# RWKV-7 recurrence of a two-block network: chunk-local products ahead of the steps, outputs in two passes

## The chip, the cores and the metric

The kernel runs on one core of a Trainium2 chip. The metric is the device time of one execution in microseconds (us), the median of several runs.

## The reference, cut to what matters

The whole program is a network of two blocks with mixture-of-experts stages for 512 tokens of 1024 features. The change touches one part, the RWKV-7 recurrence in the first mixer. For each head (8 heads of size 64) and each of two directions it is:

```python
def step(s, inp):
    r_t, w_t, k_t, v_t, kk_t, b_t = inp
    sa = jnp.einsum('dbhvk,dbhk->dbhv', s, -kk_t)
    s = s * w_t[..., None, :] + sa[..., None] * b_t[..., None, :] + v_t[..., None] * k_t[..., None, :]
    return s, jnp.einsum('dbhvk,dbhk->dbhv', s, r_t)

_, ys = lax.scan(step, s0, xs)
```

The outputs of both directions are summed, normed by group, and gated. Gated linear attention, the out projection, the experts, and the second block follow or run beside it.

## The kernel before, in words

`phase1` builds the first mixer. It treats the heads in four pairs, `rwkv_pair(0)` to `rwkv_pair(3)`, and between them it emits pieces of gated linear attention (`gl(n)`, with L608, L663, L676 and others) and of an unrelated table of modulations (`fill(n)`, with L881, L891 and L897). The code is written with a framework that plans the order of every engine's queue ahead of time: among instructions that are ready by its own estimate it prefers those emitted first. On the chip each engine then works through its queue in that order, and waits on semaphores. So pieces of attention, fill and the next pair's projections (L307) stand in TensorE's queue between the parts of a pair.

A pair is computed in 8 chunks of 64 tokens. After projections, decays and scores, a triangular solve on VectorE (L483, L484) gives `UV` (with the state-free part of U) and `W`. Then come the sums `GQ` (L532 on TensorE, L535 and L536 on VectorE), the steps over the chunks, and the outputs.

Steps (L538 to L548): state `St[n + 1]` is decay times (G times state n, plus a product of the chunk alone). For each of 7 steps n, 2 directions d and 2 heads h, L545 multiplies `RN` and `UV` with all 128 rows (tiling 128x64: 128 rows of the array, 64 columns), and L547 adds G times `St[n]` to it in the same accumulator with 64 rows (tiling 64x64). L548 on VectorE then multiplies the whole 128x128 result by the decays into `St[n + 1]`. The accumulator `pc` has the tag "ch", of which there is one PSUM bank, taken anew every four steps.

Outputs (L549 to L560): for each chunk j and head h, up to four products are added up in one bank: two of `RN` and `UV` (one for each direction, 128x64), and one or two of `GQ` and `St` (64x64). A copy on ScalarE (L560) brings them to `Y`, and the group norm, gate and transposition follow (L564 to L589). L580, also 128x64, makes the gate's projection in another bank. The tag "sc" has three banks in rotation; the sums of L532, the outputs, L580 and L585 all take theirs from it.

Tiles of one tag are handed out in the order of the program. `t2` (6 tiles) is used by a pair's preparation (first by L357) and by its end (L567, L586).

A float32 product of TensorE is two matmul instructions in the profile.

Of the kernel before, what the change touches and what calls it, by code (L numbers as in the profile page):

```python
# [14 lines left out]
OP = mybir.AluOpType  # L15
# [3 lines left out]
T, D = 512, 1024  # L19
NT, KT = 4, 8  # L20
# [3 lines left out]
# ---------------------------------------------------------------- host layout  # L24
class Cols:
    """Vectors of 128*n features as columns [128, n] of one array."""
# [14 lines left out]
def lay_out(I):  # L41
    A = {}
# [7 lines left out]
    tiles = lambda v, n: v.reshape(KT, 128, -1, n).transpose(2, 1, 0, 3)    # [column tile, partition, k, n]  # L50
# [23 lines left out]
    # ---- second block  # L74
# [21 lines left out]
    # block-diagonal gate weights, two heads a tile: [direction, r or i, tile]  # L96
# [28 lines left out]
    # constants of the shapes alone: positions, window and the transforms at the frequencies pi (2 m + 1) / 1024  # L125
    # (even positions before odd ones, and each frequency's mirror image in the second half)
# [14 lines left out]
    # rows that lie along the free dimension: [2 heads of a pair, pairs * head size]  # L141
# [6 lines left out]
# ---------------------------------------------------------------- helpers  # L148
# [15 lines left out]
class Either:  # L164
    """tiles of some tags from a pool, all others from another"""
# [8 lines left out]
class Kern:  # L174
# [9 lines left out]
    # ------------------------------------------------------------ constants  # L184
    def consts(self):
# [6 lines left out]
        # 1 where partition == column  # L192
# [10 lines left out]
        self.beforeb = p([128, 128], "beforeb", mybir.dt.bfloat16)   # 1 where partition < column  # L203
# [5 lines left out]
        self.ident2 = p([128, 64], "ident2")                         # 1 where partition % 64 == column  # L209
# [4 lines left out]
    def rstd(self, x, out, width, junk):  # L214
        """out[128, NT] = rsqrt(mean(x^2) + eps) of x [128, NT, width]"""
        nc = self.nc
        ss = self.sp([128, NT], "ss")
        for t in range(NT):
            nc.scalar.activation(junk, x[:, t], AF.Square, accum_out=ss[:, t:t + 1])
        nc.scalar.activation(ss, ss, AF.Sqrt, scale=1.0 / width, bias=self.eps)  # L220
        nc.vector.reciprocal(out, ss)

    # ------------------------------------------------------------ phase 1
    def phase1(self, _):
        """first mixer: RWKV-7 in chunks of 64, pair of heads by pair, and gated linear attention"""
# [3 lines left out]
        with ExitStack() as es:  # L229
# [15 lines left out]
            # constants of this phase  # L245
            bones = X["bones"] = P([128, 128], "bones")         # 1 where both in the same head of a pair
# [3 lines left out]
            # masks over [s, (a t | r t)], per direction: what a token takes from another of its chunk  # L250
# [10 lines left out]
            keep = P([128, 8, 64], "keep")                      # 0 at the start of every chunk  # L261
# [3 lines left out]
            omm = P([128, 15], "omm")                           # 1 - mu, mu / 2  # L265
# [3 lines left out]
            hb = X["hb"] = P([128, 16], "hb")                   # halves of the gates' biases  # L269
            V.tensor_scalar(hb, c("rw_w0_f", 0, 16), 0.5, None, op0=OP.mult)  # L270
            ka = X["ka"] = P([128, 2, 4], "ka")                 # k_a / 2, 1 - k_a / 2
# [11 lines left out]
            # ---- x, its norm, and h = rmsnorm(x) with features on partitions  # L283
# [28 lines left out]
            def shifted(ft, out):  # L312
                """out = p + mu * (centred_shift(p) - p) of feature tile ft of the projections p"""
# [32 lines left out]
    def rwkv_pair(self, i, P, bank, S, t2, bones, mask, keep, hb, ka, rw_w2, rw_a2, rw_g2, lnr,  # L346
                  shifted, wl, al, gl, **_):
        """heads 2 i and 2 i + 1, on partitions (head, n) or (direction, token), in chunks j of 64 tokens.
        The state S obeys S' = decay (S + b U + k v), U = (I - L)^-1 (a S + ka v) in each chunk."""
# [18 lines left out]
        for d in range(2):  # L368
# [4 lines left out]
            sg = t2()                                   # 2 sigmoid  # L373
# [4 lines left out]
            a = t2()                                    # tanh, of which the gate is half of 1 +  # L378
            nc.scalar.activation(a, ps, AF.Tanh, scale=0.5, bias=hb[:, 8 + 4 * d + i:9 + 4 * d + i])
            # cumulative log decays inside chunks, in the direction's order  # L380
# [26 lines left out]
        # [U; v] of direction 0, [v; U] of direction 1: tokens on partitions, [head, chunk, v]  # L407
# [11 lines left out]
        # r . k of every token times its values  # L419
# [10 lines left out]
        # scores: of the tokens a, b (and k, on the other half) on partitions; and b, k themselves  # L430
        SA, RN = [], []
        for d in range(2):
            sa, rn = S("sa", 2, 8, 64), S("rn", 2, 8, 2, 64)
            for g in range(2):
                z = slice(4 * g, 4 * g + 4)
                # (rows of one head and of the other at once, so to different banks)
# [16 lines left out]
        # [ka v | a] with tokens on partitions  # L453
# [14 lines left out]
        # (I - L)^-1 of the two 32-blocks of every unit u = (head, chunk), by substitution with units on partitions,  # L468
        # where a unit's even and odd columns lie on two; direction 1 with rows and columns reversed
# [10 lines left out]
        nc.sync.dma_start(TT, A["c_eye"])             # the identity  # L480
# [12 lines left out]
        # the block between them, and the other, of zeros  # L493
# [19 lines left out]
        # U = U0 + W S  # L513
# [10 lines left out]
        # S' = decay (G S + [b; k] [U0; v]), outputs = [.; .] [U0; v] + Q S  # L524
        GQ = S("xa", 16, 2, 64).rearrange("p (d j) a n -> p d j a n", d=2)
        for d in range(2):
            gq = GQ[:, d]
            for g in range(2):
# [7 lines left out]
                V.tensor_add(gq[:, z, 1], ps[:, :, 1], self.ident2[:, None].to_broadcast([128, 4, 64]))  # L536
        St = S("TN", 8, 2, 64)
        for n in range(7):  # L538
            if n % 4 == 0:
                pc = bank("ch").rearrange("p (n d v) -> p n d v", n=4, d=2)  # L540
            for d in range(2):
                j = 7 - n if d else n
                for h in range(2):
                    o = pc[half[h], n % 4, d]
                    nc.tensor.matmul(o, RN[d][:, h, j, 1], UV[d][:, h, j], start=True, stop=n == 0)  # L545
                    if n:
                        nc.tensor.matmul(o, GQ[half[h], d, j, 1], St[half[h], n, d], start=False, stop=True)  # L547
            V.tensor_mul(St[:, n + 1], pc[:, n % 4], DC[:, :, n:n + 1].to_broadcast([128, 2, 64]))  # L548
        Y = S("tt", 8, 64)  # L549
        ps = bank("sc").rearrange("p (j v) -> p j v", j=8)  # L550
        for j in range(8):
            for h in range(2):
                mm = [(RN[d][:, h, j, 0], UV[d][:, h, j]) for d in range(2)]
                for d in range(2):
                    n = 7 - j if d else j
                    if n:
                        mm.append((GQ[half[h], d, j, 0], St[half[h], n, d]))
                for m, (l, rhs) in enumerate(mm):
                    nc.tensor.matmul(ps[half[h], j], l, rhs, start=m == 0, stop=m == len(mm) - 1)
        nc.scalar.copy(Y, ps)  # L560
        # group norm over each head, bonus, gate
# [30 lines left out]
    def gla(self, P, bank, S, load, project, hT, gla_gw2, mask, keep, **_):  # L592
# [6 lines left out]
        def token_major(out, src, act):  # L599
            """[(head, token), chunk, 128] of the 256 columns of a pair of heads"""  # L600
# [12 lines left out]
        for i in range(2):  # L613
# [12 lines left out]
            for d in range(2):  # L626
# [5 lines left out]
                # log sigmoid(z) = min(z, 0) - ln(1 + exp(-|z|))  # L632
# [47 lines left out]
            def silu(o, p):  # L680
                """2 silu"""
# [5 lines left out]
            # states that enter each chunk  # L687
            St = S("gs", 7, 2, 128)                       # (of direction 0 without the first, of 1 without the last)
# [36 lines left out]
            # half of 2 silu: 1 / (2 rms)  # L725
# [13 lines left out]
    def residual_open(self, es, w, nb, side="right"):  # L739
        """the pool of the residual's weights w, and the first of them as pairs of float32r parts"""  # L740
# [18 lines left out]
    def residual(self, M, bank, yT, q, brow, wr, ps_, mid=lambda: None):  # L759
        """xres += gate row q * (y @ w + brow); then, tile by tile of 128 tokens, x / rms(x) as two float32r parts that  # L760
# [1146 lines left out]
```

## Time and profile before

| | us |
|---|---|
| median of 3 runs | 3128.78 |
| lowest and highest run | 3128.35, 3137.92 |
| span of the profiled execution | 3136.6 |
| TensorE (PE) busy | 2830.5 |
| VectorE (DVE) busy | 1143.0 |
| ScalarE (ACT) busy | 719.4 |
| first mixer, to the last copy of pair 3 | 724.4 |

The span runs from the first to the last instruction of one profiled execution. Busy times are sums over all instructions of an engine. PE's matmuls overlap in its pipeline and their ends are modelled, so a run of them is best read by their starts. PEclk is the TensorE clock that was granted, as a share of 2.4 GHz; 0.50 is 1.2 GHz. A row in order of time that ends in "x4" merges four instructions of one line; a bracket holds the idle time of the engine before it and what ended it.

### The profile page before, as it was taken

What the parts mean: (1) busy time and instruction counts of PE and PEld (TensorE: products, weight loads), DVE (VectorE), ACT (ScalarE), POOL (GpSimd) and SP (SyncE); (2) the same over time, 40 slices, a digit from 0 to 9 for tenths busy, and PEclk for the clock granted to TensorE, in tenths of its full rate; (3) what the DMA queues carried; (4) which work ended last, traced back from release to release, by engine and by line L of the source; (5) the groups of instructions that cost most, each with busy time, mean ns of one, the idle gap of its engine ahead of it and who ended that gap; (6) DMA issues with size and microseconds to landing.
All of it is one profiled execution on the core that took longest, in us unless ns stands there. A gap on an engine that the chain in (4) does not pass through costs nothing. (4 is left out here: it accounts for less than half of the span.)

```text
span 3136.6 us, 39504 instructions
## 1 busy us (share of the span) xinstructions
PE 2830.5 (90%) x16658; PEld 1572.0 (50%) x16658; DVE 1143.0 (36%) x1998; ACT 719.4 (23%) x1192; POOL 291.4 (9%) x265
## 2 busy tenths in 40 slices
PE   7999999867889999999889969999998886999997
PEld 3565756655545444555556653333336663333333
DVE  4756272743312222233467541112115743121112
ACT  4223122412211111244355120110104331101001
POOL 1010010102000010000245200000003230000000
PEclk9999699957889999999889979999999887999999
DMA  4245254005669787987412339999992227999987
GB/s 139 88 129 169 69 168 135 16 8 193 235 236 336 269 309 291 321 292 279 157 62 97 131 142 405 400 409 380 381 381 81 81 88 301 409 401 381 409 337 301
DMA packets 270468, 738.25 MB, mean 235 GB/s; under 512 B 14860, under 2 KB 65292, under 8 KB 269393
## 3 DMA queue, kind: packets, MB, share of 16 engines
q1 hardware_dynamic: 260480, 711.77, 60.9%
q10 hardware_dynamic: 8176, 22.27, 2.0%
q8 instruction: 132, 2.16, 0.3%
q0 software_dynamic: 1632, 1.65, 0.2%
q14 instruction: 48, 0.39, 0.0%
HBM read 727.24 MB, written 8.40 MB: 235 GB/s over the span
## 5 line engine op out<-in xcount | busy, mean ns | idle before, releaser
L1475 PE MATMUL G<-w,xT 128*64 128x256 f32 (+1 forms) x4096 | 758.3, 494 | 0.0
L1475 PEld LDWEIGHTS G<-w,xT 128*64 128x64 f32 x4096 | 279.7, 137 | 370.6 <-issue 307.5
L1495 PE MATMUL Y<-w,hT 128*64 128x512 f32 x1472 | 440.4, 600 | 0.4 <-ACT hT L1486 0.4
L1495 PEld LDWEIGHTS Y<-w,hT 128*64 128x64 f32 x1472 | 141.3, 136 | 213.7 <-issue 200.7
L1646 DVE TENSOR_TENSOR xres<-xres,cb 128x512 f32<-128x512 f32 x238 | 163.3, 686 | 207.2 <-PE cb L1644 207.0
L1480 DVE TENSOR_TENSOR h<-h,G 128x256 f32<-128x256 f32 (+1 forms) x64 | 35.5, 555 | 519.4 <-PE G L1475 394.5
L1452 PE MATMUL gat<-oh,xhi 128*128 128x256 f32 x512 | 151.5, 322 | 15.7 <-DVE oh L1666 8.7
L827 POOL TENSOR_TENSOR wl<-ws,wh 128x1024 fp32r<-128x1024 f32 x36 | 88.8, 2471 | 666.5 <-ACT wh L826 646.6
L1452 PEld LDWEIGHTS gat<-oh,xhi 128*128 128x128 f32 x512 | 102.6, 200 | 87.0 <-issue 46.3
L1635 DVE SCALAR_TENSOR_TENSOR y<-Y,gate,g 128x512 f32<-128x512 f32 x32 | 24.0, 751 | 332.1 <-PE Y L1495 330.5
L1452 PE MATMUL gat<-oh,xlo 128*128 128x256 f32 x512 | 138.4, 297 | 0.0
L1644 PE MATMUL cb<-yhi,ohT 128*128 128x512 f32 x236 | 118.8, 503 | 15.6 <-ACT yhi L1636 9.7
L1644 PEld LDWEIGHTS cb<-yhi,ohT 128*128 128x128 f32 x236 | 44.4, 188 | 152.0 <-DVE xres L1646 85.1
L307 PE MATMUL mm<-hT,w 128*128 128x512 f32 x240 | 115.9, 612 | 0.0
L1452 PEld LDWEIGHTS gat<-oh,xlo 128*128 128x128 f32 x512 | 103.5, 202 | 15.9 <-issue 14.7
L1479 ACT ACTIVATE h<-G 128x256 f32<-128x256 f32 (+1 forms) x64 | 31.4, 491 | 317.4 <-PE G L1475 317.3
L1644 PE MATMUL cb<-ylo,ohT 128*128 128x512 f32 x236 | 99.9, 423 | 3.3 <-DVE ylo L1637 2.7
L916 ACT ACTIVATE xT<-gat,mods 128x256 f32<-128x256 f32 x64 | 36.1, 564 | 247.6 <-PE gat L1452 207.4
L1182 PE MATMUL b<-big,wh 128*128 128x512 f32 x320 | 86.8, 423 | 5.0 <-ACT wh L826 2.6
L1486 ACT COPY hT<-tr 128x256 f32<-128x256 f32 (+1 forms) x64 | 30.6, 479 | 243.3 <-PE tr L1485 243.3
L881 PE MATMUL ad<-wm,sc 128*32 128x256 f32 x768 | 68.8, 401 | 12.8 <-DVE rows L892 6.1
L1636 ACT CAST yhi<-y 128x512 fp32r<-128x512 f32 x30 | 18.5, 618 | 265.6 <-DVE y L1635 167.0
(631 smaller groups left out, 4113.7 us busy)
## 6 DMA issues: line engine op xcount, KB each, us to landing
w<-in_exp_w_dram SPq DMA_DIRECT2D x384, 1024.0 KB, 13.0
w<-in_moe_w_gate_dram SPq DMA_DIRECT2D x64, 1024.0 KB, 8.0
w<-in_moe_w_up_dram SPq DMA_DIRECT2D x64, 1024.0 KB, 7.3
w<-in_moe_w_down_dram SPq DMA_DIRECT2D x56, 1024.0 KB, 6.8
wm<-in_w_mod_dram SPq DMA_DIRECT2D x96, 512.0 KB, 4.3
ws<-in_w_in_dram SPq DMA_DIRECT2D x20, 512.0 KB, 3.2
ws<-in_cf_w_dram SPq DMA_DIRECT2D x20, 512.0 KB, 3.4
st<-in_w_out_dram SPq DMA_DIRECT2D x16, 512.0 KB, 4.8
```

The source lines that it names most:

```text
L307: nc.tensor.matmul(ps[:m], w[:, k, col0:col0 + m], hT[:, k], start=k == 0, stop=k == KT - 1)
L827: self.nc.gpsimd.tensor_sub(lo, x, hi.bitcast(F32))
L881: nc.tensor.matmul(ps[32 * k:32 * k + 32, 0:256], self.sc[:, 4 * g + k], ws[g][:, k], start=g == 0, stop=g == 1)
L916: self.nc.scalar.activation(out, ps, AF.Identity, scale=a, bias=b)
L1182: nc.tensor.matmul(ps, a[:, k], b[:, k], start=m == 0 and k == 0, stop=m == 2 and k == KT - 1)
L1452: nc.tensor.matmul(ps, part[:, t, 128 * k:128 * k + 128], oh[:, t], start=t == 0 and m == 0, stop=t == NT - 1 and m == 1)
L1475: nc.tensor.matmul(parts[m][64 * c:64 * c + 64], xT[:, k, 64 * e:64 * e + 64], w[:, kk, H * c:H * c + H], start=k == 0, stop=k == KT - 1)
L1479: nc.scalar.activation(h, parts[0], AF.Silu)
L1480: nc.vector.tensor_mul(h, h, parts[1])
L1495: nc.tensor.matmul(ys[n][64 * e:64 * e + 64], hTs[e][:, f], ws[e][:, ff_, 512 * n:512 * n + 512], start=f == 0, stop=f == nf - 1)
L1644: nc.tensor.matmul(ps, ohT[:m, 128 * t:128 * t + 128], p[k][:m], start=k == 0, stop=k == 1)
L1646: V.tensor_add(xr, xr, ps)
```

## The change

The products of `RN` and `UV` of all seven steps are made first, in two banks of tag "sc", and two multiplications on VectorE put them, times their decays, into `St`. Each of the steps 1 to 6 then holds four products of `GQ` and `St`, with no accumulation across tilings, and one multiply-add on VectorE for each direction adds decay times the result to what already lies in `St[n + 1]`. `pc` is taken anew every three steps. The outputs are made in two passes with a bank each: the products of `RN` and `UV` of all chunks, copied to `Y` by ScalarE, and then the products of `GQ` and `St`, added to `Y` by VectorE. No product is added or dropped. All other differences between the two files are comments.

```diff
         St = S("TN", 8, 2, 64)
-        for n in range(7):
-            if n % 4 == 0:
+        for g in range(2):
+            ps = bank("sc").rearrange("p (n d v) -> p n d v", n=4, d=2)
+            m = range(4 * g, min(7, 4 * g + 4))
+            for n in m:
+                for d in range(2):
+                    j = 7 - n if d else n
+                    for h in range(2):
+                        nc.tensor.matmul(ps[half[h], n % 4, d], RN[d][:, h, j, 1], UV[d][:, h, j], start=True, stop=True)
+            z = slice(m[0], m[-1] + 1)
+            V.tensor_mul(St[:, m[0] + 1:m[-1] + 2], ps[:, 0:len(m)], DC[:, :, z].rearrange("p d n -> p n d")[:, :, :, None]
+                         .to_broadcast([128, len(m), 2, 64]))
+        for n in range(1, 7):
+            if n % 3 == 1:
                 pc = bank("ch").rearrange("p (n d v) -> p n d v", n=4, d=2)
             for d in range(2):
-                j = 7 - n if d else n
                 for h in range(2):
-                    o = pc[half[h], n % 4, d]
-                    nc.tensor.matmul(o, RN[d][:, h, j, 1], UV[d][:, h, j], start=True, stop=n == 0)
-                    if n:
-                        nc.tensor.matmul(o, GQ[half[h], d, j, 1], St[half[h], n, d], start=False, stop=True)
-            V.tensor_mul(St[:, n + 1], pc[:, n % 4], DC[:, :, n:n + 1].to_broadcast([128, 2, 64]))
+                    nc.tensor.matmul(pc[half[h], n % 3, d], GQ[half[h], d, 7 - n if d else n, 1], St[half[h], n, d],
+                                     start=True, stop=True)
+            for d in range(2):
+                s = St[:, n + 1, d]
+                V.scalar_tensor_tensor(s, pc[:, n % 3, d], DC[:, d, n:n + 1], s, op0=OP.mult, op1=OP.add)
         Y = S("tt", 8, 64)
         ps = bank("sc").rearrange("p (j v) -> p j v", j=8)
         for j in range(8):
             for h in range(2):
-                mm = [(RN[d][:, h, j, 0], UV[d][:, h, j]) for d in range(2)]
                 for d in range(2):
-                    n = 7 - j if d else j
-                    if n:
-                        mm.append((GQ[half[h], d, j, 0], St[half[h], n, d]))
+                    nc.tensor.matmul(ps[half[h], j], RN[d][:, h, j, 0], UV[d][:, h, j], start=d == 0, stop=d == 1)
+        nc.scalar.copy(Y, ps)
+        ps = bank("sc").rearrange("p (j v) -> p j v", j=8)
+        for j in range(8):
+            for h in range(2):
+                mm = [(GQ[half[h], d, j, 0], St[half[h], n, d]) for d, n in ((0, j), (1, 7 - j)) if n]
                 for m, (l, rhs) in enumerate(mm):
                     nc.tensor.matmul(ps[half[h], j], l, rhs, start=m == 0, stop=m == len(mm) - 1)
-        nc.scalar.copy(Y, ps)
-        # group norm over each head, bonus, gate
+        V.tensor_add(Y, Y, ps)
```

## Rows read from the trace of the kernel before

**Rows 1.** The page: span and busy time of each engine.
```profile
span 3136.6 us, 39504 instructions
...
PE 2830.5 (90%) x16658; PEld 1572.0 (50%) x16658; DVE 1143.0 (36%) x1998; ACT 719.4 (23%) x1192; POOL 291.4 (9%) x265
```

**Rows 2.** Table of stretches: us; PE, PEld, DVE, ACT, POOL busy; clock, DMA.
```profile
153.90:183.00 29.10, 29.10 (x255) 20.13 (x253) 2.18 (x10) 0.37 (x1) 0.00 (x0) 1.00 0.20 65
307.80:352.90 45.10, 45.10 (x302) 33.62 (x301) 3.13 (x8) 0.59 (x1) 0.00 (x0) 0.50 0.05 18
490.10:519.00 28.90, 28.90 (x278) 21.10 (x275) 2.07 (x8) 0.37 (x1) 0.00 (x0) 1.00 0.21 65
674.50:712.60 38.10, 36.16 (x222) 27.08 (x219) 1.75 (x6) 0.00 (x0) 0.00 (x0) 0.56 0.00 1
```

**Rows 3.** ACT in order of time: start us, us, what, idle before.
```profile
195.81 0.59 ACT L589 COPY t<-sc 128x512 f32<-128x512 f32 x1 [5.31 <-PE sc L585]
196.29 0.64 ACT L357 ACTIVATE t<-kk 128x512 f32<-128x512 f32 x1
```

**Rows 4.** PE in order of time, a step of pair 0.
```profile
156.82 0.33 PE L545 MATMUL ch<-uv,rn 128*64 128x64 f32 x2
157.08 0.32 PE L547 MATMUL ch<-TN,xa 64*64 64x64 f32 x2
...
158.88 0.64 PE L881 MATMUL ad<-wm,sc 128*32 128x256 f32 x8
```

**Rows 5.** PE in order of time, outputs of pairs 0 and 1.
```profile
171.90 0.33 PE L559 MATMUL sc<-TN,xa 64*64 64x64 f32 x2
...
173.16 0.44 PE L559 MATMUL sc<-TN,xa 64*64 64x64 f32 x4
...
182.12 0.33 PE L559 MATMUL sc<-TN,xa 64*64 64x64 f32 x2
...
183.00 0.63 PE L881 MATMUL ad<-wm,sc 128*32 128x256 f32 x6
...
334.59 0.47 PE L559 MATMUL sc<-TN,xa 64*64 64x64 f32 x2
...
336.63 0.69 PE L559 MATMUL sc<-TN,xa 64*64 64x64 f32 x4
...
351.43 0.47 PE L559 MATMUL sc<-TN,xa 64*64 64x64 f32 x2
...
352.85 7.32 PE L608 MATMUL g<-wb,hT 128*64 128x128 f32 x84
```

**Rows 6.** L580: two runs in order of time; its duration (min/median/max).
```profile
153.07 0.98 PE L580 MATMUL sc<-rw_g,lora 128*64 128x64 f32 x25
...
306.25 1.75 PE L580 MATMUL sc<-rw_g,lora 128*64 128x64 f32 x25
...
L580 PE MATMUL sc<-rw_g,lora x128: 222/222/368, 153.0 to 676.7; 128*64 128x64 f32 x128
```

**Rows 7.** PE and DVE in order of time, a step of pair 3.
```profile
690.57 0.47 PE L545 MATMUL ch<-uv,rn 128*64 128x64 f32 x2 [0.38 <-DVE TN L548]
...
693.39 0.47 PE L547 MATMUL ch<-TN,xa 64*64 64x64 f32 x2
...
693.90 0.29 DVE L548 TENSOR_TENSOR TN<-ch,DC 128x128 f32<-128x128 f32 x1 [3.39 <-PE ch L547]
```

**Rows 8.** DVE groups by line: busy us, mean ns, idle before.
```profile
L210 DVE TENSOR_TENSOR ident<-ident 128x64 f32<-128x64 f32 x1 | 0.2, 219 | 0.0
...
L548 DVE TENSOR_TENSOR TN<-ch,DC 128x128 f32<-128x128 f32 x28 | 8.1, 290 | 72.5 <-PE ch L547 72.5
...
L581 DVE TENSOR_TENSOR tt<-tt,sc 128x512 f32<-128x512 f32 x3 | 2.1, 687 | 0.1
```

**Rows 9.** Table of stretches: pair 1's clock falls and rises.
```profile
300.00:305.00 5.00, 3.51 (x56) 3.27 (x53) 2.86 (x8) 0.00 (x0) 0.49 (x1) 0.84 0.03 7
355.00:360.00 5.00, 5.00 (x68) 5.00 (x66) 1.78 (x4) 3.50 (x4) 1.40 (x2) 0.70 0.00 0
```

## Prediction

> **What bounds the kernel now.** I read the page first: TensorE (PE) is busy for 2830 of 3136.6 us [rows 1], so the question is what a change takes from PE's queue, and whether anything else would then come last. The four stretches that the change touches, one for each pair of heads, are in the table of stretches [rows 2]: 29.1, 45.1, 28.9 and 38.1 us, 141.2 us in all. In each of them PE is busy from end to end, or nearly so in the last (36.2 of 38.1), while VectorE (DVE) works about 2 us and ScalarE (ACT) under 1. PE alone sets their length. Does a shorter stretch move what follows? The square that opens the next pair's preparation (L357) starts on ACT at 196.29, straight behind the last copy of the pair before (L589, 195.81) [rows 3]: pair follows pair. Both views agree for pairs 0 to 2: PE is full, and the pairs form a chain.
>
> **Why PE is full there is seen in its order of time.** A float32 product is two instructions. In the steps, groups of two on the 128x64 tiling (L545) alternate with groups of two on 64x64 (L547). A step goes from 156.82 to 158.88 in eight groups, 0.2575 us a group [rows 4]. In the outputs (L559) groups of four alternate: 24 groups from 173.16 to 182.12, 0.373 us each [rows 5]; so two more instructions on the same tile cost 0.116 us. Where one tiling stays and only the half changes, 25 instructions of L580 take 0.98 us, of which the last one's own 0.222 us is tail: 0.0316 us each, 0.063 for two [rows 6]. The rest of a group, 0.2575 - 0.063 = 0.194 us, I call the price of a switch of tiling. Some stretches run at a granted clock of 0.50 (the level of 1.2 GHz) [rows 2]. There the same sums give 0.403 us for two (seven groups from 690.57 to 693.39), 0.617 for four (24 from 336.63 to 351.43), 0.0576 for one in a run ((1.75 - 0.368) / 24) and so 0.288 for a switch [rows 5 to 7]. A group of four without a switch is 0.063 + 0.116 = 0.179 us, at the lower level 0.115 + 0.214 = 0.329.
>
> **The change part by part.** The 224 instructions of a pair's steps and outputs stay; their order changes. So I subtract, for each pair, PE's own time after from that before.
>
> Before, at full clock: six steps of 2.06 and outputs from 171.90 to 183.00 make 12.4 + 11.1 = 23.5 us; the other 5.6 us of the stretch is fill (L580, L881 and others between the steps). At the lower level: 6 x 3.23 + 18.3 (334.59 to 352.85) = 37.7 us, with 7.4 of fill in pair 1.
>
> After, at full clock: the 24 products of the six steps in one run, 24 x 0.063 = 1.5; six steps of four groups, each with a switch in and one out because fill stands between steps, 6 x (4 x 0.063 + 2 x 0.194) = 3.8; first output pass, 16 groups of four, 2.9; second pass, 12 of four and four of two, 2.4; two more switches 0.4. Sum 11.0 us, a gain of 12.5 for each of pairs 0 and 2. At the lower level the same line gives 2.8 + 6.2 + 5.3 + 4.4 + 0.6 = 19.2, a gain of 18.5 for pair 1, if its clock is again at 0.50.
>
> DVE work added per pair: twelve 128x64 multiply-adds out of PSUM for six 128x128 multiplies, two scalings of all states in place of the first multiply, and an addition of 128x512 where ACT had a copy. No row has the 128x64 form from PSUM. The bounds are 0.219 us (128x64 between SBUF tiles, L210) and 0.290 (twice as wide, from PSUM, L548) [rows 8]; I take 0.21 for each of the two, 0.42 a step, nearest to the narrow row, since following DVE instructions overlap a little (pairs of 0.29 would be 0.58). The scaling is like L581, 0.687 us for 128x512. The final addition is of the same size, for an ACT copy of 0.59 (like L589 [rows 3]): 0.1 us, left out. In pairs 0 to 2 all this is hidden by fill, as DVE is free for 27 of 29 us; without that cover a step would be the chain below, 0.95 instead of 0.64, and each pair would lose 1.9 us.
>
> The Trainium skill, "VectorE: DVE Perf Modes", section "Rules for kernel authors", speaks against this part: it asks for as few chained DVE instructions as can be, since each flushes the pipe. By it alone every one of the 24 steps would pay the extra 0.13 us, 3 us in all, and the sum below would be 64 instead of 66.
>
> Pair 3 has no fill left, so its steps are a chain. Before, L545 waits 0.38 us for the multiply of the step before although its own operands are ready [rows 7]: writes to the bank wait for its reader. After, PE's four groups at full clock last 7 x 0.0316 + 0.222 = 0.44 us, then 0.04 to DVE (693.86 to 693.90), 0.42 there, and 0.05 back (what 0.38 leaves beside 0.04 and the multiply's 0.29): 0.95 us; at the lower level 1.28. With 0.69 for the first scaling, six steps, what of the first pass and its two switches is not covered by that scaling, the second pass and a tail: 0.7 + 5.7 + 2.6 + 2.4 + 0.3 = 11.7 us at full clock, 0.7 + 7.7 + 5.2 + 4.4 + 0.7 = 18.6 at the lower. The clock of this stretch was 0.56 on the mean [rows 2], with full clock in its first microseconds; I take the middle, 15.2, a gain of 22.9. What is late next is the tail of norms, the same as before.
>
> What else moves: the run of products needs two more "sc" banks of three in rotation. They come free as DVE reads the sums of G and Q, so a bank is there before the 0.69 us scaling ends; I put this at nothing, at most one scaling (0.7 us) a pair. No DMA is added. The loads queued on SP and the small ones on POOL keep their places, as no instruction of those queues is in the edited lines; stages behind start earlier as a whole.
>
> Sum: 12.5 + 18.5 + 12.5 + 22.9 = 66.4 us. The profiled execution, 3136.6 us, becomes 3070.2. It is 7.8 us longer than the median of the runs shown, 3128.78; less the same 7.8, the prediction is 3062 us.
>
> **The rivals.**
> Pair 1 at full clock. Its clock fell in 300:305, where PE was busy for 3.51 of 5 us, and came back in 355:360, behind the run of L608 from 352.85 [rows 5, 9]. The new order puts long runs of one tiling right behind the fall. Then 45.1 us become 11.0 + 7.4 x 0.0316 / 0.0576 = 15.1, a gain of 30.0: 11.5 more, 3051 us.
> Pairs 0 and 2 at the lower clock. Their alternating groups held 1.00 [rows 2]; with more of PE's time in waits for DVE they may not. Each gains 23.5 - 19.2 = 4.3 instead of 12.5, 16.4 us less: 3079 us. [...]
> Only the last pair counts. If PE's time in pairs 0 to 2 is only traded for waits at the solves on DVE, 23 us are left: 3106 us. For it: PE has room in later parts of pair 3; against it: PE is full through the stretches and L357 follows L589.
> The order doesn't come about. The planner fills each queue by readiness, and could weave the first pass between the L547 groups; then the switches stay: within 0.3% of 3128. Against it: L580 runs 25 at a time already [rows 6].
> Slower: the lower clock spreads. If the thinner steps drop the clock and it stays down through the dense projections and fill behind, their time doubles. It decides once 66 us of dense full-clock work runs at half; with two stretches of 40 us between pairs the time is 3062 + 80 = 3142 us. Against it: in 355:360 the clock rose within a few microseconds of dense work [rows 9].
>
> **How the numbers follow.** Forecast 0.45 (3062), pair 1 at full clock 0.20 (3051), pairs 0 and 2 at the lower 0.15 (3079), only the last pair 0.10 (3106), order not there 0.05 (3128), slower 0.05 (3142). The first four are all faster by more than 0.3% (9.4 us, about what a measurement of this kernel can tell from no change): 0.90; same 0.05; slower 0.05. The range takes in the first three with their bounds. Low: 3051, less 3.5 (pair 3 all at full clock), less 7 (step switches absent in pairs 0 to 2, 18 x 0.39), less 6 for waits such as the 1.5 us one of 300:305, one a pair: 3034. High: 3079, plus 3.4 (pair 3 all at the lower level), plus 3.8 (24 steps with 0.58 on DVE), plus the same 6: 3092. It leaves out 0.20.
>
> **What would show it.** In the changed profile the two output passes should be blocks of about 3 and 2.5 us at full clock, the L547 groups of a step should start 0.06 us apart, the four stretches should last some 17, 27, 16 and 15 us, and the last copy of pair 3 (L589, which ends at 724.4 now) should end near 658. The prediction is wrong if groups of one tiling still cost 0.25 us (then the switch is not the price), if PE waits between pairs grow by what the stretches lose, or if the granted clock is at 0.50 in stretches where it was 1.00.

## The result, and the profile after

The kernel after takes 3042.21 us (median of four runs, 3040.67 to 3054.99); the kernel before, run beside it, 3128.57 (median of four, 3118.65 to 3137.92). The ratio is 0.9737 with a 95% interval of 0.9699 to 0.9775: 86.4 us less (70 to 94). The forecast was 3062 with a range of 3034 to 3092. The profiled executions, on which the sums of the prediction rest, stand further apart: 3136.6 against 3041.3 us of span, 95.3. Fifteen more runs of the kernel before lie between 3109 and 3144 us: the five with a mean granted clock of 0.940 or more took 3109 to 3121, the other ten (0.932 to 0.937) 3123 to 3144; the profiled one of before (0.933) is among the slower.

The page of the kernel after, span and busy times, which answers to [rows 1]:

```profile
span 3041.3 us, 39560 instructions
PE 2735.9 (90%) x16658; PEld 1507.6 (50%) x16658; DVE 1153.3 (38%) x2030; ACT 719.2 (24%) x1192; POOL 292.1 (10%) x265
```

PE has as many instructions as before, 16658, and is busy for 94.6 us less; the span is 95.3 us shorter. DVE works 10.3 us more. Lines are a little further down in this kernel: products ahead L548, their scaling L550, products of a step L557, multiply-add L561, first output pass L567, second L574, its addition L575, gate L595 (was L580), last copy of a pair L604 (was L589), fill L896 (was L881).

The table of the four stretches (us; PE, PEld, DVE, ACT, POOL busy; clock, DMA), which answers to [rows 2]:

```profile
153.90:165.90 12.00, 12.00 (x217) 8.10 (x214) 4.39 (x19) 0.98 (x3) 0.00 (x0) 1.00 0.26 89
288.60:302.40 13.80, 13.09 (x250) 9.28 (x246) 8.73 (x24) 3.42 (x6) 0.00 (x0) 1.00 0.26 79
432.60:444.50 11.90, 11.90 (x260) 9.56 (x256) 4.41 (x16) 0.96 (x2) 0.00 (x0) 1.00 0.27 90
604.00:615.10 11.10, 9.37 (x198) 8.23 (x194) 4.09 (x14) 0.58 (x1) 0.00 (x0) 0.80 0.01 3
```

They were 29.1, 45.1, 28.9 and 38.1 us and are 12.0, 13.8, 11.9 and 11.1: 17.1, 31.3, 17.0 and 27.0 less, 92.4 in all. The windows don't hold quite the same work: 0.9 to 1.3 us of the products ahead lie in front of each of these, and in front of those of before lie the first step's products and most of the gate (1.2 us in pair 0, from 152.67; 2.2 in pair 1, from 305.60), so each difference is good to about 1 us. Read the clock too: it is at 1.00 in pair 1 and at 0.80 in pair 3, where it was 0.50 and 0.56.

PE in order of time through pair 0, which answers to [rows 4] and [rows 5] (start us, us, what):

```profile
152.57 1.85 PE L548 MATMUL sc<-uv,rn 128*64 128x64 f32 x56
154.26 0.28 PE L567 MATMUL sc<-uv,rn 128*64 128x64 f32 x2
154.52 0.45 PE L557 MATMUL ch<-TN,xa 64*64 64x64 f32 x8
154.90 0.92 PE L567 MATMUL sc<-uv,rn 128*64 128x64 f32 x24
...
163.90 1.90 PE L574 MATMUL sc<-TN,xa 64*64 64x64 f32 x56
165.72 0.98 PE L595 MATMUL sc<-rw_g,lora 128*64 128x64 f32 x26
```

What were alternating groups of four, 0.373 us each, are now runs of one tiling. The 56 instructions of the second pass are one run, which starts 1.82 us before what follows it: 0.030 us each with a last one of 0.222. The 64 of the first pass are no single block: the planner put them between the first four steps, as runs of 2, 24, 22 and 16.

ACT around the end of pair 0, which answers to [rows 3]:

```profile
177.79 0.58 ACT L604 COPY t<-sc 128x512 f32<-128x512 f32 x1 [3.46 <-PE sc L600]
178.28 0.63 ACT L357 ACTIVATE t<-kk 128x512 f32<-128x512 f32 x1
```

Still pair follows pair: L357 stands straight behind the last copy, now 18 us earlier. The last copy of pair 3 ends at 627.2 instead of 724.4, 97.2 us earlier, and the end of the kernel gets 95.3 of them.

PE and DVE in pair 3, which answers to [rows 7]:

```profile
608.44 0.45 PE L557 MATMUL ch<-TN,xa 64*64 64x64 f32 x8
608.93 0.47 DVE L561 SCALAR_TENSOR_TENSOR TN<-ch,DC,TN 128x64 f32<-128x64 f32 x2 [0.63 <-PE ch L557]
609.46 0.45 PE L557 MATMUL ch<-TN,xa 64*64 64x64 f32 x8 [0.57 <-DVE TN L561]
...
610.49 0.66 PE L557 MATMUL ch<-TN,xa 64*64 64x64 f32 x8 [0.58 <-DVE TN L561]
...
611.71 3.31 PE L574 MATMUL sc<-TN,xa 64*64 64x64 f32 x56 [0.57 <-DVE TN L561]
```

This is the chain that was foreseen: eight instructions 0.45, 0.04 to DVE, two multiply-adds 0.47, 0.06 back: 1.02 us a step. The second pass, at the lower clock by then, takes 3.2 us.

### The profile page after: what moved, and what is told of

Same layout as the page of the kernel before. It is cut to its first block, busy times and chain, and to the rows that moved or that the text cites. A ratio compares the mean times of both kernels' runs of the same rounds, so it can differ in the third digit from the quotient of the medians.

```text
span 3041.3 us, 39560 instructions
## 1 busy us (share of the span) xinstructions
PE 2735.9 (90%) x16658; PEld 1507.6 (50%) x16658; DVE 1153.3 (38%) x2030; ACT 719.2 (24%) x1192; POOL 292.1 (10%) x265
## 5 line engine op out<-in xcount | busy, mean ns | idle before, releaser
L896 PE MATMUL ad<-wm,sc 128*32 128x256 f32 x768 | 66.2, 402 | 12.6 <-DVE rows L907 6.3
```

Of the source, the lines that this page charges most:

```text
L896: nc.tensor.matmul(ps[32 * k:32 * k + 32, 0:256], self.sc[:, 4 * g + k], ws[g][:, k], start=g == 0, stop=g == 1)
```

## Experiments

Theory: what the change takes away is switches of tiling in PE's queue, and the clock of pair 1 and of pair 3 with them. Rivals: half of the change does all of it; it is the accumulation of both kinds of products in one bank that costs, not the switch; the clock of pair 1 is an accident of one execution; another order of the fill does as much.

### One half at a time

The steps of the kernel after with the outputs of the kernel before:

```diff
-        for j in range(8):
-            for h in range(2):
-                for d in range(2):
-                    nc.tensor.matmul(ps[half[h], j], RN[d][:, h, j, 0], UV[d][:, h, j], start=d == 0, stop=d == 1)
-        nc.scalar.copy(Y, ps)
...
+                mm = [(RN[d][:, h, j, 0], UV[d][:, h, j]) for d in range(2)]
+                for d in range(2):
+                    n = 7 - j if d else j
+                    if n:
+                        mm.append((GQ[half[h], d, j, 0], St[half[h], n, d]))
```

> Edit: the changed kernel with the outputs of the kernel before (one bank, groups of four that alternate between 128x64 and 64x64); products ahead and steps as in the changed kernel. Theory (the price lies in alternating tilings, wherever they alternate): each pair's outputs take 11.1 us at full clock again instead of 3.9, so some 7 us a pair more than the changed kernel, and about 12 where the clock is at 0.50: 3070 to 3085 us. Rival (the gain comes from the steps alone, because products no longer queue behind the reader of their bank): within 5 us of the changed kernel, 3042 us.

3077.65 us (3077.03 to 3078.32), ratio 0.985 (0.9811 to 0.9888). Its table of stretches:

```profile
154.00:175.60 21.60, 21.60 (x248) 14.57 (x246) 4.14 (x18) 0.37 (x1) 0.00 (x0) 1.00 0.26 86
298.00:317.70 19.70, 19.70 (x284) 14.99 (x280) 4.84 (x16) 0.96 (x2) 0.00 (x0) 1.00 0.22 68
443.20:463.50 20.30, 20.30 (x268) 15.43 (x266) 3.89 (x16) 0.37 (x1) 0.00 (x0) 1.00 0.20 66
624.80:650.00 25.20, 22.67 (x206) 17.98 (x202) 3.61 (x14) 0.01 (x1) 0.00 (x0) 0.63 0.00 1
```

The other way round, the steps of the kernel before with the outputs of the kernel after (the reverse diff, for the steps):

> Edit: the kernel before with the outputs of the changed kernel (two passes of one tiling each); steps with accumulation across tilings as before. Theory (alternating tilings): outputs of 11.1 us become 3.9 in pairs 0 and 2, of 18.3 become 6 to 7 in pairs 1 and 3: 3128 - 14 - 24 = 3090 us, and some 15 us less if pair 1 runs at full clock. Rival (the steps alone): within 5 us of 3128.

3071.23 us (3068.25 to 3083.13), ratio 0.984 (0.9795 to 0.9884). Its table of stretches:

```profile
156.50:176.00 19.50, 19.50 (x211) 13.45 (x210) 2.18 (x10) 0.96 (x2) 0.00 (x0) 1.00 0.17 55
296.00:314.90 18.90, 18.90 (x223) 14.31 (x224) 2.50 (x7) 3.73 (x5) 0.00 (x0) 0.95 0.00 1
450.20:468.80 18.60, 18.60 (x224) 13.88 (x224) 2.08 (x8) 0.96 (x2) 0.00 (x0) 1.00 0.19 58
624.20:644.80 20.60, 19.45 (x188) 14.99 (x188) 1.75 (x6) 0.59 (x1) 0.00 (x0) 0.73 0.01 2
```

Set against [rows 2], the steps bring 7.5 and the outputs 9.6 in pair 0; together that is the 17.1 of the whole change (each to about 1 us, as above). In pair 2 it is 8.6 and 10.3 (17.0 by the whole), in pair 3 12.9 and 17.5 (27.0). In pair 1 they bring 25.4 and 26.2, but the whole only 31.3: some 20 us stand in both. That is the clock. Either half alone had pair 1 at full clock, or nearly (0.95), and it can be gained only once. So both halves count, and a part of pair 1's gain doesn't hang on which switches went: with the old outputs, too, its clock was not down.

### Switch or accumulation

The kernel after with both passes in their own banks and with their own copy and addition, but their groups in turn, as the outputs of the kernel before had them:

```diff
+        p1, p2 = (bank("sc").rearrange("p (j v) -> p j v", j=8) for _ in range(2))
...
         for j in range(8):
             for h in range(2):
+                with (self.tc.issue_after(last) if last is not None else ExitStack()):
+                    for d in range(2):
+                        x = nc.tensor.matmul(p1[half[h], j], RN[d][:, h, j, 0], UV[d][:, h, j], start=d == 0, stop=d == 1)
...
+                with self.tc.issue_after(x.ins):
+                    for m, (l, rhs) in enumerate(mm):
+                        last = nc.tensor.matmul(p2[half[h], j], l, rhs, start=m == 0, stop=m == len(mm) - 1).ins
```

> Edit: the changed kernel with both output passes kept in their own banks, with the same copy and addition behind them, but queued so that a group of the first pass and a group of the second alternate. Nothing but the order on TensorE is undone. Theory (alternating tilings): groups of four take 0.37 us at full clock, the outputs 11 us instead of 1.95 + 1.90; 7 us a pair more than the changed kernel at full clock, about 14 for a pair at 0.50: 3070 to 3085 us. Rival (accumulating both kinds of product in one bank was what cost time): groups take 0.12 to 0.18 us and the time is within 8 us of 3042.

3080.09 us (3073.43 to 3085.24), ratio 0.9859 (0.9816 to 0.9901): with the steps alone changed it was 3077.65, so the two passes brought nothing that shows in this order. PE in order of time in pair 0:

```profile
168.24 0.45 PE L569 MATMUL sc<-uv,rn 128*64 128x64 f32 x4
168.62 0.44 PE L573 MATMUL sc<-TN,xa 64*64 64x64 f32 x4
168.99 0.45 PE L569 MATMUL sc<-uv,rn 128*64 128x64 f32 x4
```

Its table of stretches, the groups of pairs 0 and 3:

```profile
166.60:177.80 11.20, 11.20 (x119) 9.10 (x120) 1.50 (x2) 0.92 (x2) 0.00 (x0) 1.00 0.24 78
634.50:652.90 18.40, 18.35 (x118) 14.71 (x120) 0.00 (x0) 0.39 (x1) 0.00 (x0) 0.50 0.00 1
```

The groups start 0.373 us apart, as in [rows 5], and the outputs take 11.2 and 18.4 us as they did, though no product is added to one of another tiling any more. In the outputs the price is the alternation of tilings; for the steps the next run shows the same. The Trainium skill, "TensorEngine Tiling (Array Packing)", section "Key Properties", says that a change of tiling mode drains the TensorE; these rows agree in that each change costs time, and put a size to it.

### What a group costs, by its length

The kernel after with products of constants ahead of the first mixer, results unused: alternating groups of two, a straight run of one tiling, groups of two again, a run, groups of four on one half, a run, groups of eight with the halves in turn, a run.

```diff
+            wide = lambda h: nc.tensor.matmul(scratch[z[h], 0:64], bones[:, z[h]], bones[:, 0:64], start=True, stop=True)
+            square = lambda h: nc.tensor.matmul(scratch[z[h], 64:128], bones[z[h], z[h]], bones[z[h], 0:64], start=True, stop=True)
...
+            alternate(80, lambda g: [g % 2])
+            for g in range(160):
+                nc.tensor.matmul(scratch[z[g % 2], 128:192], bones[:, z[g % 2]], bones[:, 0:64], start=True, stop=True)
+            alternate(120, lambda g: [g % 2])
...
+            alternate(80, lambda g: [g % 2, g % 2])
...
+            alternate(40, lambda g: [0, 1, 0, 1])
```

> Edit: the changed kernel with products of constants at the start of the first mixer, into a bank that nobody reads; the rest is unchanged, and the time longer by the added run (some 100 us). In order: 80 groups of two instructions that alternate between 128x64 and 64x64; 320 instructions on 128x64 alone, changing the half at every product; 120 alternating groups of two; 240 on 128x64; 80 alternating groups of four; 240 on 128x64 with four on the same half in a row; 40 alternating groups of eight with four changes of half; 240 on 64x64. Theory (a price for each switch): at full clock 0.26 us for a group of two, 0.37 for four, 0.38 for eight; the runs 0.03 us an instruction. My prediction's price list says that four in a row on the same half cost 0.179 us; the changed kernel's first pass (24 in 0.85 us) says 0.12. Clock: if alternating groups by themselves neither raise nor lower the clock, the first 20 us stay at 0.50, and the later alternating stretches at 1.00; if they let it fall, the second alternating stretch (31 us) ends at 0.50; if they raise it like any product, the first stretch is at 1.00 after some microseconds.

PE in order of time (wide L252, square L253, straight runs L262 and L268), cut out of the middle of each part:

```profile
39.80 1.39 PE L262 MATMUL sc<-bones 128*64 128x64 f32 x42
...
46.83 0.33 PE L252 MATMUL sc<-bones 128*64 128x64 f32 x2
47.08 0.33 PE L253 MATMUL sc<-bones 64*64 64x64 f32 x2
...
109.97 0.44 PE L253 MATMUL sc<-bones 64*64 64x64 f32 x4
110.34 0.45 PE L252 MATMUL sc<-bones 128*64 128x64 f32 x4
...
132.79 1.39 PE L268 MATMUL sc<-bones 128*64 128x64 f32 x42
...
144.80 0.45 PE L253 MATMUL sc<-bones 64*64 64x64 f32 x8
145.18 0.45 PE L252 MATMUL sc<-bones 128*64 128x64 f32 x8
```

And the table of stretches of the same kernel: the second part with groups of two, from its start and later, and the groups of four:

```profile
45.00:50.00 5.00, 5.00 (x41) 3.69 (x40) 0.00 (x0) 0.00 (x0) 0.00 (x0) 1.00 0.01 3
55.00:90.00 35.00, 35.00 (x176) 24.79 (x178) 0.00 (x0) 0.00 (x0) 0.00 (x0) 0.50 0.00 1
100.00:128.00 28.00, 28.00 (x301) 22.91 (x302) 0.00 (x0) 0.00 (x0) 0.00 (x0) 1.00 0.01 2
```

At full clock an alternating group of two starts 0.257 us before the next (twenty of them from 45.03 to 50.16), one of four (on one half) 0.373, one of eight (halves in turn) 0.38. Nothing is accumulated here, and the groups of two take what they took in the steps before (0.2575): there, too, it was the alternation that cost. In a run an instruction takes (1.39 - 0.222) / 41 = 0.0285 us, and it is the same when four in a row lie on one half (L268). So the 0.116 us for two more on the same tile, which the prediction read from [rows 4, 5], is no property of the tile: it shows only between switches. Second, the clock. Steady groups of two, with PE busy for 35.00 of 35.00 us, went from 1.00 to 0.50 within some microseconds and stayed there; groups of four held 1.00 for 28 us. At the start of this execution the clock column can't be used: it reads 1.00 there, while the first eighty groups of two start 0.403 us apart (from 19.80 to 21.01 in three), the pace that goes with 0.50 later. By its starts the straight run of L262 behind them began at 0.055 us an instruction (34.32) and went at 0.0285 from about 37 us on. The products of constants make the total, 3178.81 us, no comparison.

### Why pair 1 stood at the lower clock

The kernel before with twelve dense products, results unused, ahead of pair 1's steps (`last` is the last product of L532):

```diff
+        if i == 1:
+            dummy = bank("ch")
+            with self.tc.issue_after(last.ins):
+                for _ in range(12):
+                    nc.tensor.matmul(dummy, ident, v, start=True, stop=True)
```

> The kernel before, and in pair 1 alone twelve dense products more (identity times v, 128x128 by 128x512, 24 instructions, results unused) in TensorE's queue behind the last sum of L532 and ahead of the steps. Such an instruction takes about 0.434 us at full clock, so they add 10.4 us at full clock and 20.8 at the lower one. The question is why the steps and outputs of pair 1 ran at a granted clock of 0.50 for 45 us before. Theory: the clock had fallen in the waits ahead of them, and groups of two that alternate with another tiling do not raise it again; a dense run ahead raises it, and then, as in pairs 0 and 2, the same instructions hold 1.00. It expects the granted clock at 1.00 in pair 1's steps and outputs, some 28 us for them instead of 45.1, the dense run itself 11 to 14 us, and a total 3 to 6 us below the kernel before. Rival: the alternating groups of two pull the clock down again within a few microseconds, as in the run of constants where they fell back to 0.403 us a group; then the stretch keeps some 40 to 45 us at 0.50 and the total is 8 to 13 us above the kernel before.

A single execution, 3123.86 us, beside runs of before from 3109 to 3144, so the total says little. Its steps and outputs in the table of stretches:

```profile
315.90:344.00 28.10, 28.07 (x324) 21.71 (x325) 3.24 (x9) 0.12 (x1) 0.00 (x0) 1.00 0.09 29
```

45.1 became 28.1 us with not one switch fewer: the clock alone was worth 17 us. But the dense products didn't have to raise it. PE's wait ahead of them was shorter this time and the clock was never down, so what is shown is that the old order holds full clock if it enters with it. What it does once the clock is down, and what the new order does, the next two ask: the same 80 groups of two, of constants, ahead of pair 1 in the kernel after and in the kernel before.

```diff
+        if i == 1:
+            dummy = bank("ch")
+            with self.tc.issue_after(last.ins):
+                for g in range(80):
+                    h = half[g // 2 % 2]
+                    w = ident[h] if g % 2 else ident
+                    nc.tensor.matmul(dummy[h, 64 * (g % 2):64 * (g % 2) + 64], w[:, h], bones[h, 0:64] if g % 2 else bones[:, 0:64], start=True, stop=True)
```

> The kernel after, and in pair 1 alone 80 groups of constants (results unused) behind the last sum of L532 and ahead of the products of the steps: groups of two 128x64 instructions that alternate with groups of two 64x64, as in the kernel before. They cost 80 x 0.2575 = 20.6 us at full clock and 80 x 0.403 = 32 at the lower one, and, by the run of constants, leave the granted clock at 0.50. The question is what the new order does when its stretch begins at the lower clock, which in the kernel after it never did. Theory: its runs of one tiling raise the clock as the straight runs of constants did, so that the 56 products of the steps still go at about 0.058 us each, and the rest of the stretch, or nearly all of it, at 1.00: 14 to 18 us for a stretch that took 13.8 at full clock. Rival: the steps between the runs hold it at the lower level, as the old order did for 45 us; then the stretch takes 24 to 28 us. The total is no evidence, some 20 to 30 us above 3042.

> The counterpart: the same 80 groups of constants at the same place of pair 1 in the kernel before. Theory: the steps and outputs that follow, with their alternating groups, stay at the lower clock from the first group to the last, some 45 us; the stretch of the kernel before was no accident of one execution, but what its order does once the clock is down. Rival: the fill between the steps raises the clock within the stretch, which then takes some 30 to 38 us.

The kernel after with them, PE in order of time (constants L547, products ahead L555, first pass L574), and then two rows of its table of stretches, of which the second goes from the first product to the last of the second pass:

```profile
282.39 30.79 PE L547 MATMUL ch<-bones,ident 128*64 128x64 f32 x160
313.11 3.06 PE L555 MATMUL sc<-uv,rn 128*64 128x64 f32 x56
316.00 0.28 PE L574 MATMUL sc<-uv,rn 128*64 128x64 f32 x2
```

```profile
315.00:320.00 5.00, 5.00 (x123) 4.53 (x121) 2.61 (x8) 0.19 (x1) 0.00 (x0) 0.92 0.02 3
...
313.10:327.90 14.80, 14.80 (x309) 11.78 (x308) 5.24 (x16) 1.52 (x3) 0.00 (x0) 0.91 0.23 71
```

The kernel before with them, the table of stretches from the first step to the last output:

```profile
332.30:377.10 44.80, 44.80 (x314) 33.86 (x313) 3.25 (x9) 0.00 (x0) 0.00 (x0) 0.50 0.06 18
```

This settles what either order does with a clock that is down. From the same lower clock the old order stays at 0.50 for 44.8 us, to its last group, and the new one is out of it within its 56 straight instructions (0.50 to 315.5, 1.00 from 316.0) and needs 14.8 us.

It doesn't settle why the clock was down in one kernel and not in the other. In the kernel before it fell at 303.5, within the last run of L532, which had begun behind a wait of 1.49 us; neither the rest of that run nor the 25 straight instructions of L580 [rows 6] raised it again:

```profile
302.18 3.49 PE L532 MATMUL sc<-rn,Lu 64*64 64x128 f32 x46 [1.49 <-DVE Lu L523]
```

In the kernel after the clock fell ahead of pair 1 too, as its table of stretches has it:

```profile
275.00:280.00 5.00, 2.94 (x48) 2.12 (x46) 2.24 (x6) 1.52 (x5) 0.87 (x1) 0.95 0.40 141
280.00:285.00 5.00, 5.00 (x40) 2.93 (x40) 1.51 (x4) 1.53 (x5) 0.48 (x1) 0.71 0.78 264
285.00:290.00 5.00, 4.83 (x122) 4.48 (x124) 4.49 (x11) 3.23 (x4) 0.48 (x1) 1.00 0.02 3
```

It answers to [rows 9]: the fall came earlier, and the clock was back at 1.00 by 283, some 4 us ahead of the first product ahead (287.39), while PE was at work on instructions that the order before has too. So in this execution it wasn't the new order that brought it back, and whether and when it falls there is not shown to depend on the order; what the new order changes is that a fall no longer costs the whole stretch. Only one execution of the kernel before was profiled. An estimate from [rows 2]: 45.1 us at 0.50 take 45.1 x 0.5 / 3136.6 = 0.007 off an execution's mean clock, which is about what parts 0.933 from 0.940 among the runs listed with the result. Beside an execution whose pair 1 holds full clock, as in the run with dense products, some 17 us of the gain would be missing. The Trainium skill, "TensorE: Matmul & The Clock Gate", section "Why this matters for your kernels", warns of idle gaps between bursts. Here PE was busy for 44.80 of 44.80 us at 0.50: without a gap in the profile, too, the clock can be down, where short groups of two tilings alternate.

### One bank or two in pair 3

```diff
-                pc = bank("ch").rearrange("p (n d v) -> p n d v", n=4, d=2)
+                pc = [bank(t).rearrange("p (n d v) -> p n d v", n=4, d=2) for t in ("ch", "ad" if i == 3 else "ch")[:1 + (i == 3)]]
...
```

> The kernel after, with the step accumulators of direction 1 in a bank of their own in pair 3 alone. A step of pair 3 took 1.02 us (starts 608.44, 609.46, 610.49), with TensorE idle for 0.57 until the second of the two multiply-adds ended. Theory: the next step's first product writes into the bank that the multiply-add of direction 1 still reads, so it waits for both; with two banks the products of direction 0 start when the first multiply-add has ended, and a step lasts about 0.75 us, pair 3's six steps 1.5 us less. Rival: it is the state that each direction needs and the turn-round between the engines, not the bank, and a step stays at 1.0 us. The total can show neither, 1.5 of 3042 us; the starts of the steps can.

PE in pair 3 in order of time:

```profile
609.63 0.33 PE L557 MATMUL ch<-TN,xa 64*64 64x64 f32 x4
609.89 0.33 PE L567 MATMUL sc<-uv,rn 128*64 128x64 f32 x2
610.15 0.33 PE L557 MATMUL ad<-TN,xa 64*64 64x64 f32 x4
...
610.79 0.33 PE L557 MATMUL ch<-TN,xa 64*64 64x64 f32 x4
```

A step takes 1.16 us here (from the first group in "ch" at 609.63 to the next at 610.79; the others 1.10 to 1.29), not 0.75 and not 1.0. With the directions apart the planner puts products of the first pass between them, so that a step has four switches instead of two, and no step is left that shows the bank alone. What the bank costs stays open; the attempt only shows how easily the switches come back. The time was 3042.37 us.

### Another order of the fill

In the kernel after TensorE is busy for 17.7 of the 40 us around pair 3's solve (560 to 600). Two kernels move the twelve pieces of fill ahead of pair 3, all or six of them, to the end of the phase, where the planner may draw them forward (shown is the one with six; the other leaves the line out):

```diff
-            fill(12)
+            fill(6)
```

> The kernel after, with the twelve pieces of the modulation table that are emitted ahead of pair 3 left to the end of the phase, so that they can lie beside pair 3's solve, steps and norms. In the kernel after TensorE has nothing for about 40 us around pair 3's solve (busy 0 of 5 us in 575:580 and 580:585, the clock at 0.50 from 560 on) and for its tail. Theory: the pieces (12 x 16 wide products of 128x256 and their sums, near 25 us of TensorE) fill these gaps, pair 3's whole chain starts earlier, and the total falls by 10 to 20 us, to 3022 to 3032. Rival: the DVE, ACT and DMA work of the pieces gets in between pair 3's chain, or the pieces run behind pair 3 anyway, and the total stays within 5 us of 3042 or rises.

> As the run with twelve pieces late, but six of the twelve stay ahead of pair 3. Theory: half of the gain, 5 to 10 us, unless what counts is only that the gap around the solve is filled, for which six pieces (some 12 us of TensorE) are enough; then it gains as much as twelve. Rival: no gain, 3042 within 5 us.

All twelve late: 3061.01 us (3058.59 to 3064.58), ratio 0.9794 (0.9736 to 0.9852), some 19 us slower than the kernel after. PE in order of time (fill L895, first product of the out projection L788):

```profile
613.75 1.08 PE L895 MATMUL ad<-wm,sc 128*32 128x256 f32 x8 [2.21 <-DMA wm<-in_w_mod_dram]
...
655.44 0.77 PE L788 MATMUL G<-wh,yh 128*128 128x512 f32 x1 [12.08 <-ACT yh L840]
```

Pair 3 does end sooner, but the fill runs on until 643.4, waiting for its loads and for ACT and DVE, and the out projection begins at 655.44 instead of 636.58. Six late: 3035.98 us (3035.07 to 3044.35), ratio 0.9719 (0.9661 to 0.9778). There the fill is through at 590.7, inside the solve, and the out projection begins at 630.7, 5.9 us earlier. That is the size of the difference to the kernel after (6.2 us), but the two intervals overlap, so that it isn't shown to be faster.

## Why the prediction was right, and where it was off

**The bound.** Right. PE's busy time and the span fell by the same (94.6 and 95.3 us), L357 still starts behind the last copy, and of the 97.2 us at the last copy of pair 3 95.3 reached the end. Behind the outputs of pair 3 stands the tail of norms as before: from 615.1 to the last copy's end at 627.2 it is 12.1 us, and was 11.8.

**The switch as the price.** Right as the cause, shown by the woven passes and by the groups of constants; its size was off, in two terms. Pair 0's own PE time was to be 11.0 us and is 8.4:

| us in pair 0 | prediction | starts in the trace after |
|---|---|---|
| products ahead (24 priced, 28 made) | 1.5 | 1.7 |
| six steps | 3.8 | 2.3 |
| first pass | 2.9 | 2.6 |
| second pass | 2.4 | 1.8 |
| two more switches | 0.4 | in the rows above |

A step's eight instructions and the switch behind them take 0.38 (154.52 to 154.90): less 8 x 0.030 that is 0.14 for a switch beside a longer block, where the prediction took 0.194 from groups of two. And a group of four on one half costs 4 x 0.030 = 0.12 in a run, not 0.179. The steps' other switches, out of the first pass and the fill, stand in the first pass's 2.6 us and in the fill. So pair 0 gained 15.1, not 12.5 (the fill, 5.6 before, is 4.75), and pair 2 is its like.

**Pair 1.** The step that failed is "if its clock is again at 0.50". The pair was at 1.00, as the rival with a chance of 0.20 had it, and the stretch is 13.8 us where that rival said 15.1. That rival's reason was long runs of one tiling behind the fall. The two runs with 80 groups show that the new order does so, but in the profiled execution of the kernel after the clock was back before the first of these runs. So the number came out for a reason other than the one given, and that this execution entered pair 1 at full clock is luck as far as the runs show. Of the 31.3 us about 17 are the clock (45.1 to 28.1 in the old order) and about 14 the order.

**Pair 3.** The mechanism was right to a few hundredths: a step at full clock 1.02 for 0.95, and 0.05 of the difference is the two multiply-adds on DVE, 0.47 for 0.42. The sum was off: 11.1 us instead of 15.2. The first pass, 2.6 to 5.2 us in the sum, costs 0.5, as it stands in the waits of the first three steps (1.23, 1.22 and 1.12 us instead of 1.02), and the clock stayed at 1.00 until the last step (0.56 in 610.40:611.70). The second pass, 3.2 us, lies between its two prices.

**VectorE.** Right. In pairs 0 and 2 PE is busy from end to end (12.00 of 12.00 us), so the chained multiply-adds cost nothing there; in pair 1 PE waited once for the first scaling (0.15 us), and in pair 3 they cost 0.05 a step. The rule of the Trainium skill, "VectorE: DVE Perf Modes", section "Rules for kernel authors", to keep chained DVE instructions few, would have taken 2 us off the gain by the prediction's price of it: the total is too coarse to show that, but the rows of pairs 0 and 2, in which PE waits for no multiply-add, show none of it there.

**The sum put right.** From one profiled execution to the other the stretches gave 17.1 + 31.3 + 17.0 + 27.0 = 92.4 us, the time between them 5.1, and what stands behind pair 3's outputs took 2.2 more: 95.3, where the prediction's sum was 66.4. It had nothing for the time between the stretches. From pair 1's to pair 2's it went from 137.2 to 130.2 us, at a granted clock of 0.97 instead of 0.93; from pair 2's to pair 3's it rose from 155.5 to 159.5, and no run asked why. So the rows were short by 28.9 us and the forecast by 20, because one more term was off: the span before stood 7.8 us above the median, the prediction took off the same 7.8 after, and there the span stands 0.9 below it. That 3062 comes as near as it does is in part luck; 3042 lies in the range because the low end took in pair 1 and pair 3 at full clock.

**The marks named ahead.** They came out on the same side. The L557 groups of a step start 0.065 us apart for two (0.06 expected), the second pass is a block of 1.8 us (2.5), the stretches are shorter still than the 17, 27, 16 and 15 us, and the last copy ends at 627 instead of 658. The first pass takes 2.6 us (3) but is no block: the planner did weave it between the steps, as a rival had feared, only in runs so long that few switches came back. None of the rivals that would have made it 3079 or more showed: pairs 0 and 2 stayed at 1.00.

## What to carry to other kernels

Where products of two tilings alternate, count the switches in PE's queue rather than the products, and give each tiling its own block, even at the price of a bank and an addition on an engine with time to spare. Read the granted clock of each stretch before pricing it, and ask what brings it back: an order that needs luck to be at full clock is worth less than its best execution. And look at the queue again after every small edit, as a planner that fills waits can weave the tilings together again.

## What the runs showed of the hardware

- A busy PE was no guard of the clock: steady alternating groups of two let the granted clock fall from 1.00 to 0.50 without any idle time in the profile, and it stayed there (35 us of constants; 44.8 us of pair 1, with groups of four and short runs of fill among them). With fill between the steps the same groups held 1.00 in pairs 0 and 2 [rows 2]. Groups of four held 1.00, but at 0.50 they didn't raise it [rows 5]. Of the straight runs some did (within the 56 instructions of the products ahead it was back) and some did not (L532 and L580 ahead of pair 1 in the kernel before).
- The time of an alternating group isn't a fixed switch plus its instructions: 0.257 us for two, 0.373 for four on one half, 0.38 for eight with the halves in turn, against 0.0285 for an instruction in a run. Eight cost what four did.
- Two 128x64 multiply-adds out of PSUM, one behind the other, took 0.47 to 0.48 us; one alone 0.28.
